# Issuing the transfers of an RWKV pair's turn from SyncE or ScalarE, by the planner's choice

## The chip, the cores and the metric

The kernel runs on one core of one Trainium2 chip. The metric is the device time of the whole program in microseconds, as the median of several runs; lower is better. The engines are TensorE (PE, with its weight load PEld), VectorE (DVE), ScalarE (ACT), GpSimd (POOL) and SyncE (SP). SyncE does no arithmetic; in the kernel before, it issues every data transfer.

## The reference

One inference step of one decoder layer, for a prompt of 1024 tokens and 8 sample tokens, width 1024, all in float32. The input is projected by `w_in`; two branches (gated linear attention with 4 heads, and RWKV-7 with 16 heads of 64) run a recurrence over the tokens; their outputs are projected, gated, added, projected again and normalized. The part that matters here is the RWKV-7 recurrence:

```python
def step(S, inp):
    rt, wt, kt, vt, kkt, at = inp
    sa = jnp.einsum('bhvk,bhk->bhv', S, -kkt)
    S = S * wt[:, :, None, :] + sa[..., None] * (kkt * at)[:, :, None, :] + vt[..., None] * kt[:, :, None, :]
    y = jnp.einsum('bhvk,bhk->bhv', S, rt)
    return S, y
...
p = jnp.einsum('btd,dn->btn', x, w_in)
...
m = (jax.nn.sigmoid(gate_a) * jnp.einsum('btc,cd->btd', o_gla, w_up_gla)
     + jax.nn.sigmoid(gate_b) * jnp.einsum('btc,cd->btd', o_rwkv, w_up_rwkv))
out = jnp.einsum('btd,de->bte', m, w_out)
y_out = _layernorm(DEEPNORM_ALPHA * x + out, ln_g, ln_b, LN_EPS)
```

## The kernel before

**Passes and blocks.** The prompt is worked in two passes (`PASS`, line 29): 512 tokens with the 8 sample tokens (as columns 256 + 264), then 512 tokens. In each pass, `blocks` (line 689) projects `w_in` block by block, 128 output columns at a time: 24 products for each column tile (8 slices of the width, each in three parts of a split into high and low halves), into one of two PSUM banks named `proj`. When the 24 are done, ScalarE or VectorE empties the bank (`evacuate`, line 730). The weights come as `wraw`, are split into `wpart` by ScalarE and VectorE, are stored in DRAM (`w`) and come back as `wpart` in the second pass. In the trace nearly every instruction has line 219, since one helper records them, so instructions are told apart by their tiles.

**A pair's turn.** The 16 RWKV heads go in 8 pairs per pass, 16 turns in all (`pair`, line 1075). The recurrence is done in chunks of 64 tokens, which needs the inverse of a triangular matrix for each chunk and head. `front` (line 1099) forms the products `GG` (tile `gg`), and then:

1. four transfers store the diagonal 32 x 32 blocks of `gg` to DRAM (`LD`, line 1178), four bring them back as one block per partition (`wide<-LD`, line 1186);
2. VectorE solves all blocks together, 62 small instructions over `X` and `Xt`;
3. four transfers store the solution (`XD<-X`, line 1198); four take off-diagonal blocks of `gg` into `L1` (shown as `L<-gg`, line 1207); four bring the solution into `XT` (line 1212) and four into `X2` (shown as `X<-XD`, line 1216). The last two need `XD` to have landed;
4. `back` (line 1219) transposes on VectorE (`X<-XT`) and takes two small products on TensorE (`big<-X,L` and `big<-X,A`) for the off-diagonal part.

That makes 24 transfers per pair, 384 in all. Then `chain` (line 1264) walks through the 8 chunks in order, with three products each on TensorE (`pch`) and copies between them on ScalarE and VectorE, and `norm` normalizes the pair's output.

**What sets the order.** All work is written as streams of operations, and `run` (line 373) acts as a list scheduler while the program is built. It keeps a clock for each engine, estimates the start of every stream's next operation (`start`, line 336) from prices (`price`, line 147) and from when its inputs are ready, and takes the one with the smallest start time less a priority. An `Engine` object (line 208) with several engines gives an operation several ways, of which `start` takes the one that ends first; `self.C` (ScalarE or VectorE) and `self.E` (VectorE or GpSimd) are of that kind. Each engine's instructions then run on the chip strictly in the order in which they were recorded, and a waiting instruction holds up all that stand behind it on its engine. A transfer is priced at 0.56 us of SyncE's clock, and its landing is estimated by `transfer` (line 202). All transfers go through `self.S`, SyncE alone.

Of the kernel before, what the change touches and what calls it, by code (L numbers as in the profile page):

```python
# [20 lines left out]
P = 128  # L21
D = 1024
# [11 lines left out]
NCH = HT // C  # L34
# [34 lines left out]
SWITCH = 0.09  # L69
# [6 lines left out]
LANDED = 0.5  # L76
BIAS = 0.1
ASIDE = 0.5

PRIO = {"evacuate": 0.7, "pair": 0.4, "turn": 0.5, "chain": 0.5, "norm": 0.1, "x": 0.7, "lora": 0.2, "rank": -0.3,  # L80
        "head": 0.3, "gate": 0.05, "w": 0.3, "out": -0.1, "state": 0, "block": 0.0}
# [7 lines left out]
HS = (slice(0, 64), slice(64, 128))  # L89
# [57 lines left out]
def price(eng, name, out, args, ins):  # L147

    n = out.free_size()
    src = [x for x in ins if x.tensor.space != PSUM] if eng == "A" else ins  # L150
    if eng == "P":
        m = args[0].free_size()
        rows, cols = tiles(name, args)
        if name == "transpose":
            return 0.112 * rows / P
        if args[0].dtype == F32R:
            return max(m / 1200, n / 2165)
        if rows == cols == P:
            return 2 * max(m, n) / 1200 + 0.005
        return 2 * (max(m, n) if cols == P else m + n) / 1200 * min(0.5 if cols == P else 0.25, rows * cols / P ** 2) + (0.01 if cols == P else 0.0)  # L160
    if eng == "S":
        return 0.56
    if eng == "A":
        extra = len(ins) - 1
        return 0.097 + n / 1200 + (0.042 if len(src) == len(ins) else 0.0) + 0.094 * extra
    wide = max([n, *(x.free_size() for x in ins)]) if name in ("tensor_reduce", "bn_stats", "bn_aggr") else n
    if eng == "V":
        if name == "tensor_tensor_scan":
            return 0.1 + n / 480
        if name in ("tensor_copy", "copy", "memset") and ins and ins[0].tensor.space != PSUM:  # L170
            wide = wide / 2
        scalars = sum(x.free_size() == 1 for x in ins[1:]) if name in ("scalar_tensor_tensor", "tensor_scalar") else 0
        return 0.068 + wide / (480 if name == "copy_predicated" else 960) + 0.06 * scalars
    if name in ("tensor_scalar", "memset"):
        return 0.08 + n / 760
    return 0.1 + n / (300 if name == "tensor_copy" else 456)
# [31 lines left out]
class Engine:  # L208
# [3 lines left out]
    def __getattr__(self, name):  # L212
        def make(out, *args, **kw):
            ins = [x for x in (*args, *kw.values()) if isinstance(x, AP)]
            ways = []
            lag, table, part, port = 0.0, None, None, ""
            for eng, handle in self._handles.items():
                call = getattr(handle, "tensor_copy" if (eng, name) == ("V", "copy") else name)
                ways.append((eng, lambda call=call: call(out, *args, **kw), price(eng, name, out, args, ins)))  # L219
                if eng in "VG" and shared(eng, name, out, ins):  # L220
                    port += eng
            if eng == "S":
                lag = transfer(out, args[0])
            elif eng == "A" and name == "activation":
                table = SETS.get(args[1])
            elif eng == "P":
                part = tiles(name, args)
            return Op(ways, out, ins, lag, table, part, port)
        return make
# [22 lines left out]
class Order:  # L252
# [4 lines left out]
    def __init__(self, nc):  # L257
        self.P, self.A, self.V, self.G, self.S, self.E, self.C = (Engine(**e) for e in (
            {"P": nc.tensor}, {"A": nc.scalar}, {"V": nc.vector}, {"G": nc.gpsimd}, {"S": nc.sync},
            {"V": nc.vector, "G": nc.gpsimd}, {"A": nc.scalar, "V": nc.vector}))  # L260
        self.tiles = (P, P)
        self.quads = {"V": {}, "A": {}}
        self.time = dict.fromkeys("PAVGS", 0.0)
        self.port = dict.fromkeys("VG", 0.0)
        self.dma = 0.0
        self.table = EXP
        self.ready, self.read = {}, {}
        self.streams = []
        self.idle, self.make, self.home, self.wait = {}, {}, {}, {}
        self.kept, self.tile = {}, {}  # L270
# [65 lines left out]
    def start(self, op):  # L336

        best = None
        for eng, fn, cost in op.ways:
            free, t = self.time[eng] + (SWITCH if eng == "P" and op.tiles != self.tiles else 0.0), 0.0  # L340
            for x in (*op.outs, *op.ins):
                at, by = self.ready.get(x.tensor.name, (0.0, None))
                if eng == "S" and by == "D" and x is op.out:
                    continue
                if by != eng:
                    at += HOP.get(by, 0.0) + (SPARE if eng == "P" and by in ("V", "A", "G") else LANDED if by == "D" else 0.0)
                elif eng != "P" and x is not op.out:
                    at += 0.13
                t = max(t, at)
            t = max(t, *(self.read.get(x.tensor.name, 0.0) for x in op.outs))  # L350
            if eng in op.port:
                free = max(free, self.port["G" if eng == "V" else "V"])
            late, t = free - t, max(t, free)
            if eng in "VA" and self.held(eng, op):
                cost += HOLD
            end = t + cost
            if len(op.ways) > 1:
                end += BIAS if eng == "V" and "A" in op.ways[0][0] else ASIDE if eng == "G" and "G" in op.port else 0.0
            if best is None or end < best[0]:
                best = end, t  # L360
                op.eng, op.fn, op.cost, op.late = eng, fn, cost, max(0.0, late)
        return best[1]
# [10 lines left out]
    def run(self):  # L373
        while self.streams:
            best, before = None, list(self.streams)
            self.urgent = self.needed()
            for s in before:
                self.advance(s)
                if s.op is not None:
                    t = self.start(s.op)  # L380
# [10 lines left out]
            _, t, s = best  # L391
            op, s.op = s.op, None
            cost = op.cost
# [2 lines left out]
                self.table = op.table  # L396
                self.nc.scalar.preload_act_table_set(self.table)  # L397
            op.fn()
            self.time[op.eng] = max(self.time[op.eng], t + cost)
            if op.eng in op.port:  # L400
                self.port[op.eng] = t + cost
            if op.eng == "P":
# [2 lines left out]
                for x, q in self.starts(op):  # L405
                    self.quads[op.eng][x is op.out, x.space] = q
            end = t + cost
            if op.eng == "S":
                self.dma = max(self.dma, end) + op.lag[0]
                end = self.dma + op.lag[1]  # L410
            for x in op.outs:
                n = x.tensor.name
                self.ready[n] = max(end, self.ready.get(n, (0.0,))[0]), "D" if op.eng == "S" else op.eng
            for x in op.ins:
                n = x.tensor.name
                self.read[n] = max(self.read.get(n, 0.0), end)
# [2 lines left out]
class Kern(Order):  # L419
# [679 lines left out]
    def front(self, c, p, st, d):  # L1099
        a, A, V, E = self.a, self.A, self.V, self.E  # L1100
        BK_, L_ = (yield from self.get("bk")), (yield from self.get("wide"))
# [3 lines left out]
        GG = gg.rearrange("p (c k h t) -> p c k h t", c=NCH, k=2, h=2)  # L1105
# [56 lines left out]
        H = NCH // 2  # L1162
# [10 lines left out]
        NU = 4 * NCH  # L1173
        LD = self.dr.tile([4, NCH, 32, 32], F32, name=f"LD{c.i}{p}")
        for q in range(2):
            b = slice(32 * q, 32 * q + 32)
            for h in range(2):
                yield self.S.dma_start(LD[2 * q + h].rearrange("c s t -> s c t"), GG[HS[h]][b, :, 0, h, b])
        L = L_.rearrange("p (s t) -> p s t", t=32)
        X_ = yield from self.get("X")  # L1180
        X = X_.rearrange("p (i t) -> p i t", t=32)
# [1 line left out]
        for q in range(4):  # L1183
            yield E.memset(X_[NU * q:NU * q + NU, q::36], 1.0)
        for q in range(4):
            yield self.S.dma_start(L_[NU * q:NU * q + NU], LD.rearrange("n c s t -> (n c) (s t)"))
        tm = yield from self.get("Xt")
        for j in range(31):
            w, ni = 31 - j, j // 4 + 1
# [5 lines left out]
        XT = (yield from self.get("XT")).rearrange("p (c h t) -> p c h t", c=NCH, h=2)  # L1195
        XD = self.dr.tile([4 * NCH, 32, 32], F32, name=f"XD{c.i}{p}")
        for q in range(4):
            yield self.S.dma_start(XD.rearrange("u (i g) t -> g u i t", g=4)[q], X[NU * q:NU * q + NU])
        self.free(X_)

        L1 = (yield from self.get("L1")).rearrange("p (x t) -> p x t", t=32)
# [1 line left out]
        H = NCH // 2  # L1203
        for h in range(2):
            for n in range(2):
                g = 2 * h + n
                yield self.S.dma_start(L1[32 * g:32 * g + 32], GG[64 * h:64 * h + 32, H * n:H * n + H, 0, h, 32:64])
        for q in range(2):
            b = slice(32 * q, 32 * q + 32)
            for h in range(2):  # L1210
                n = 2 * q + h
                yield self.S.dma_start(XT[HS[h]][b, :, h, b], XD[n * NCH:(n + 1) * NCH].rearrange("c s t -> s c t"))

        for x in range(H):
            b = slice(32 * x, 32 * x + 32)
            yield self.S.dma_start(X2[b, :, b], XD[2 * NCH + x::H].rearrange("g s t -> s g t"))
        d.AZ, d.BK, d.G, d.XT, d.v, d.bonus, d.pc, d.L, d.L1, d.X2 = AZ, BK, GG, XT, st[2], st[1], pc, L_, L1, X2

    def back(self, d):
# [577 lines left out]
```

## Time and profile before

| | |
|---|---|
| median of 3 runs | 1496.26 us (1493.49 to 1500.5) |
| the profiled execution | 1493.88 us, of which the span from first to last instruction is 1492.1 us |
| TensorE's granted clock, mean | 0.998 |
| transfers moved | 319.01 MB, mean 214 GB/s |

In the profile, a busy engine is one that executes an instruction; register and semaphore instructions and the issue of a transfer are not counted as busy. Rows with `SPq` are SyncE's issues, with the time that the issue took SyncE (not the transfer). A row "A <- B: us, times, longest" says that an instruction of engine A sat idle until one of B ended. In rows of a window, the busy time of PE, PEld, DVE, ACT and POOL is followed by the granted clock, the DMA engines' busy share and the GB/s moved.

### The profile page before, as it was taken

The page shows a single profiled execution, that of the slowest core. Times are in us where ns is not written, and L with a number is a line of the kernel's source. Part 1 is how long each engine was busy: PE and PEld are TensorE (multiplying, and loading weights), DVE is VectorE, ACT ScalarE, POOL GpSimd, SP SyncE. Part 2 cuts the span into 40 slices and gives each one's busy share as a digit, 9 for nine tenths or more (in the row PEclk, how much of TensorE's full clock was granted, in tenths as well). Part 3 has the DMA queues.
Part 4 walks back from the last instruction along what each step waited for, and adds up shares of the span by engine and source line. Part 5 has one row for each costly group of instructions (what it writes and reads, how often), then busy time and mean ns, then how long its engine had stood idle before and what let it go on. Part 6 is the DMA issues. An engine that isn't in the chain of part 4 may idle for free.

```text
span 1492.1 us, 30560 instructions
## 1 busy us (share of the span) xinstructions
PE 1466.4 (98%) x10678; PEld 1282.5 (86%) x10678; DVE 1201.9 (81%) x3159; ACT 880.1 (59%) x2221; POOL 115.5 (8%) x217
## 2 busy tenths in 40 slices
PE   9999999999999999999999999999999999999997
PEld 6998999999999999787877887787788899988786
DVE  6697889988998898979887998888777876756665
ACT  6665767767677677565754556465646746644210
POOL 1001002101120002001001010101000000000000
PEclk9999999999999999999999999999999999999999
DMA  9876697668767877675566565656554768887432
GB/s 310 282 267 207 221 314 227 218 220 302 234 220 221 297 239 241 185 237 168 165 203 175 161 199 180 181 154 171 177 172 135 234 197 258 282 300 264 143 106 85
DMA packets 211253, 319.01 MB, mean 214 GB/s; under 512 B 91683, under 2 KB 107180, under 8 KB 211100
## 3 DMA queue, kind: packets, MB, share of 16 engines
q1 hardware_dynamic: 211100, 317.06, 66.6%
q8 instruction: 85, 1.39, 0.4%
q14 instruction: 68, 0.56, 0.1%
HBM read 197.32 MB, written 118.61 MB: 212 GB/s over the span
## 4 chain that ended last, share of the span: by engine, by line
PE 83%; DVE 7%; DMA 4%; ACT 2%; issue 1%; SPq 1%; POOL 0%; POOLq 0%; DVEq 0%; ACTq 0%
PE proj L219 51%; PE big L219 22%; PE pch L219 6%; PE pY L219 5%; DVE row L219 2%; SPq L219 1%; DMA row<-o_rwkv 1%; ACT row L219 1%; DMA wraw<-w_in 1%; DVE X L219 1%; DVE wpart L219 1%; DMA wide<-LD 1%; DMA row<-state_rwkv 1%; DVE Xt L219 0%; ACT L397 0%
## 5 line engine op out<-in xcount | busy, mean ns | idle before, releaser
L219 PE MATMUL proj<-xs,wpart 128*128 128x264 f32 (+2 forms) x5640 | 1028.6, 327 | 1.2 <-DVE row L219 0.8
L219 PEld LDWEIGHTS proj<-xs,wpart 128*128 128x128 f32 x5640 | 814.4, 189 | 80.8 <-issue 10.3
L219 ACT CAST wpart<-wraw 128x512 fp32r<-128x512 f32 x210 | 130.2, 623 | 84.1 <-PE big L219 31.0
L219 DVE TENSOR_TENSOR wpart<-wraw,wpart 128x512 fp32r<-128x512 f32 x205 | 142.5, 697 | 33.4 <-ACT wpart L219 30.2
L219 DVE TENSOR_TENSOR row<-row 128x512 f32<-128x512 f32 (+10 forms) x295 | 156.8, 536 | 10.9 <-DMA row<-state_rwkv 6.2
L219 ACT ACTIVATE row<-row 128x512 f32<-128x512 f32 (+4 forms) x229 | 138.6, 610 | 26.2 <-DVE row L219 13.8
L219 POOL TENSOR_TENSOR row<-row 128x256 f32<-128x256 f32 (+7 forms) x74 | 70.3, 955 | 669.5 <-DVE row L219 232.9
L219 DVE TENSOR_TENSOR Xt<-X,wide 128x60 f32<-128x60 f32 (+24 forms) x496 | 108.4, 218 | 15.4 <-DMA wide<-LD 2.7
L219 DVE TENSOR_TENSOR X<-X,Xt 128x60 f32<-128x60 f32 (+24 forms) x496 | 106.0, 214 | 12.0
L219 ACT ACTIVATE row<-proj,omu 128x256 f32<-128x256 f32 (+1 forms) x99 | 54.3, 549 | 72.2 <-PE proj L219 71.8
L219 PE MATMUL big<-xs,wpart 128*128 128x512 f32 (+2 forms) x552 | 93.5, 324 | 0.0
L219 PEld LDWEIGHTS big<-xs,wpart 128*128 128x128 f32 x552 | 81.1, 188 | 8.7
L219 PE MATMUL big<-row 128*128 128x128 f32 (+4 forms) x464 | 86.6, 317 | 0.3 <-DVE Xt L219 0.3
L397 ACT ACT_TABLE_LOAD x64 | 82.1, 1283 | 1.1
L219 DVE SCALAR_TENSOR_TENSOR wide<-pch,pc,s0p 64x64 f32<-64x64 f32 x208 | 58.5, 281 | 28.3 <-PE pch L219 23.9
L219 DVE SCALAR_TENSOR_TENSOR row<-proj,pv,row 128x255 f32<-128x255 f32 (+1 forms) x99 | 56.3, 569 | 30.2 <-ACT tail L219 23.0
L219 ACT COPY row<-wide 64x64 f32<-64x64 f32 x240 | 57.9, 241 | 32.7 <-DVE wide L219 25.2
L219 ACT COPY wide<-pch 64x64 f32<-64x64 f32 x165 | 34.2, 207 | 65.1 <-PE pch L219 63.7
L219 PEld LDWEIGHTS big<-row 128*128 128x128 f32 (+3 forms) x464 | 60.5, 175 | 8.2 <-ACT row L219 0.8
L219 ACT COPY row<-big 128x128 f32<-128x128 f32 (+7 forms) x140 | 39.9, 313 | 41.7 <-PE big L219 40.4
L219 ACT ACTIVATE row<-proj 128x128 f32<-128x128 f32 (+4 forms) x136 | 36.9, 324 | 31.2 <-PE proj L219 30.5
L219 PE MATMUL big<-part,headsr 128*128 128x512 f32 x128 | 53.4, 418 | 1.7 <-DVE part L219 1.7
(234 smaller groups left out, 2025.8 us busy)
## 6 DMA issues: line engine op xcount, KB each, us to landing
w<-wpart SPq DMA_DIRECT2D x146, 512.0 KB
wpart<-w SPq DMA_DIRECT2D x146, 512.0 KB
wraw<-w_in SPq DMA_DIRECT2D x146, 256.0 KB
wide<-LD SPq DMA_DIRECT2D x64, 128.0 KB
wraw<-w_up_gla SPq DMA_DIRECT2D x32, 256.0 KB
wraw<-w_up_rwkv SPq DMA_DIRECT2D x32, 256.0 KB
sg<-row SPq DMA_DIRECT2D x16, 260.0 KB
row<-sg SPq DMA_DIRECT2D x16, 260.0 KB
```

The lines of the kernel that those rows point to most:

```text
L219: ways.append((eng, lambda call=call: call(out, *args, **kw), price(eng, name, out, args, ins)))
L397: self.nc.scalar.preload_act_table_set(self.table)
```

## The change

The six groups of transfers of a pair's turn are now made through `self.B`, which has two ways: `S` is SyncE's queue and `Q` is ScalarE's. The way `Q` is priced at 0.45 us on ScalarE's clock (SyncE keeps 0.56), and for the choice 0.3 us (`ASIDE_Q`) is added to its end. Whichever ends sooner by this estimate issues the transfer. Landing is estimated as before, with one shared clock of the DMA engines for both. All other transfers stay on SyncE.

```diff
+ASIDE_Q = 0.3
...
-    if eng == "S":
-        return 0.56
+    if eng in "SQ":
+        return 0.56 if eng == "S" else 0.45
...
+        self.Q = Engine(Q=nc.scalar)
+        self.B = Engine(S=nc.sync, Q=nc.scalar)
...
-            free, t = self.time[eng] + (SWITCH if eng == "P" and op.tiles != self.tiles else 0.0), 0.0
+            free, t = self.time["A" if eng == "Q" else eng] + (SWITCH if eng == "P" and op.tiles != self.tiles else 0.0), 0.0
...
-                end += BIAS if eng == "V" and "A" in op.ways[0][0] else ASIDE if eng == "G" and "G" in op.port else 0.0
+                end += ASIDE_Q if eng == "Q" else BIAS if eng == "V" and "A" in op.ways[0][0] else ASIDE if eng == "G" and "G" in op.port else 0.0
...
-            self.time[op.eng] = max(self.time[op.eng], t + cost)
+            clock = "A" if op.eng == "Q" else op.eng
+            self.time[clock] = max(self.time[clock], t + cost)
...
-            if op.eng == "S":
+            if op.eng in "SQ":
                 self.dma = max(self.dma, end) + op.lag[0]
                 end = self.dma + op.lag[1]
...
-                yield self.S.dma_start(LD[2 * q + h].rearrange("c s t -> s c t"), GG[HS[h]][b, :, 0, h, b])
+                yield self.B.dma_start(LD[2 * q + h].rearrange("c s t -> s c t"), GG[HS[h]][b, :, 0, h, b])
...
-            yield self.S.dma_start(L_[NU * q:NU * q + NU], LD.rearrange("n c s t -> (n c) (s t)"))
+            yield self.B.dma_start(L_[NU * q:NU * q + NU], LD.rearrange("n c s t -> (n c) (s t)"))
...
-            yield self.S.dma_start(XD.rearrange("u (i g) t -> g u i t", g=4)[q], X[NU * q:NU * q + NU])
+            yield self.B.dma_start(XD.rearrange("u (i g) t -> g u i t", g=4)[q], X[NU * q:NU * q + NU])
...
-                yield self.S.dma_start(L1[32 * g:32 * g + 32], GG[64 * h:64 * h + 32, H * n:H * n + H, 0, h, 32:64])
+                yield self.B.dma_start(L1[32 * g:32 * g + 32], GG[64 * h:64 * h + 32, H * n:H * n + H, 0, h, 32:64])
...
-                yield self.S.dma_start(XT[HS[h]][b, :, h, b], XD[n * NCH:(n + 1) * NCH].rearrange("c s t -> s c t"))
+                yield self.B.dma_start(XT[HS[h]][b, :, h, b], XD[n * NCH:(n + 1) * NCH].rearrange("c s t -> s c t"))
...
-            yield self.S.dma_start(X2[b, :, b], XD[2 * NCH + x::H].rearrange("g s t -> s g t"))
+            yield self.B.dma_start(X2[b, :, b], XD[2 * NCH + x::H].rearrange("g s t -> s g t"))
```

Since the planner decides, the whole order is made anew. Of the 384 transfers, 168 come to stand on ScalarE and 216 stay on SyncE; the other 947 transfers stay on SyncE too. ScalarE has 61 table loads in place of 65, and 36 copies that it did stand on VectorE now. TensorE has the same 9106 matrix instructions in another order.

The first place is SyncE's queue at the seventh pair of the second pass, after its solve; `wpart<-w` are weights that come back. Before:

```order
715 L219 DMA wpart<-w_1_8439 128x1024
716 L219 DMA wpart<-w_0_8476 128x1024
717 L219 DMA XD_15594<-X 256x1x32 x4
718 L219 DMA L_15619<-gg 32x4x32 x4
719 L219 DMA XT_167<-XD_15594 32x8x32 x4
720 L219 DMA X_173<-XD_15594 32x4x32 x4
721 L219 DMA wpart<-w_1_8528 128x1024
```

And now:

```order
705 L220 DMA wpart<-w_0_8363 128x1024
706 L220 DMA XD_15540<-X 256x1x32 x2
707 L220 DMA L_15551<-gg 32x4x32 x2
708 L220 DMA wpart<-w_1_8471 128x1024
709 L220 DMA XT_167<-XD_15540 32x8x32 x2
710 L220 DMA X_173<-XD_15540 32x4x32 x2
711 L220 DMA wpart<-w_0_8533 128x1024
```

Half of each group has left the queue, and a load of weights stands between `L` and `XT`.

The second place is ScalarE's queue at the same pair. `row<-proj,omu`, `tail<-proj` empty a projection bank, `part<-row` is the high half of a split for a head sum on TensorE. Before:

```order
1474 L219 COPY row<-row 128x256
1475 L219 ACTIVATE row<-row 128x512
1476 L219 CAST part<-row 128x512
1477 L219 COPY row<-row 128x256
1478 L219 COPY row<-big 64x2x64 x2
1479 L219 COPY row<-big 128x384 x2
1480 L219 ACTIVATE row<-proj,omu 128x512
```

And now:

```order
1543 L220 COPY tail<-proj 128x1
1544 L220 ACTIVATE row<-carry,row,pv 128x1
1545 L220 DMA XD_15540<-X 256x1x32 x2
1546 L220 DMA L_15551<-gg 32x4x32 x2
1547 L220 DMA XT_167<-XD_15540 32x8x32 x2
1548 L220 DMA X_173<-XD_15540 32x4x32 x2
1549 L220 ACTIVATE row<-row 128x512
1550 L220 ACTIVATE row<-proj,omu 128x512
1551 L220 COPY tail<-proj 128x1
1552 L220 COPY row<-row 128x256
1553 L220 CAST part<-row 128x512
```

Eight issues stand together ahead of the square, the emptying of a bank and the cast; the fifth of them must wait until `XD` has landed.

The third place is ScalarE's queue at the fourth pair of the first pass, now (before, it held no transfers); `wpart<-wraw` is the split of weights:

```order
487 L220 DMA XD_5031<-X 256x1x32 x2
488 L220 ACTIVATE row<-proj,omu 128x264
489 L220 COPY carry<-proj 128x1
490 L220 COPY tail<-proj 128x8
491 L220 DMA L_5049<-gg 32x4x32
492 L220 ACTIVATE row<-bnd,row,pv 128x1
493 L220 COPY smp<-row 128x8
494 L400 ACT_TABLE_LOAD
495 L220 ACTIVATE row<-big,pv 128x512 x2
496 L220 ACTIVATE row<-proj 128x128 x2
497 L220 DMA XT_168<-XD_5031 32x8x32
498 L220 CAST wpart<-wraw 128x512
```

Here ScalarE's other work stands between the issues, the emptying of a bank among it.

More of the change, by code (lines that the diff above doesn't have):

```diff
@@ L221, in make @@
                     port += eng
-            if eng == "S":
+            if eng in "SQ":
                 lag = transfer(out, args[0])
@@ L339, in start @@
         for eng, fn, cost in op.ways:
-            free, t = self.time[eng] + (SWITCH if eng == "P" and op.tiles != self.tiles else 0.0), 0.0
+            free, t = self.time["A" if eng == "Q" else eng] + (SWITCH if eng == "P" and op.tiles != self.tiles else 0.0), 0.0
             for x in (*op.outs, *op.ins):
                 at, by = self.ready.get(x.tensor.name, (0.0, None))
-                if eng == "S" and by == "D" and x is op.out:
+                if eng in "SQ" and by == "D" and x is op.out:
                     continue
@@ L412, in run @@
                 n = x.tensor.name
-                self.ready[n] = max(end, self.ready.get(n, (0.0,))[0]), "D" if op.eng == "S" else op.eng
+                self.ready[n] = max(end, self.ready.get(n, (0.0,))[0]), "D" if op.eng in "SQ" else op.eng
             for x in op.ins:
```

## The prediction

> **What bounds the kernel now.** I read the page's first part, then busy time by stage, then what TensorE waits for, then SyncE's rows around one turn.
>
> ```profile
> span 1492.1 us, 30560 instructions
> PE 1466.4 (98%) x10678; PEld 1282.5 (86%) x10678; DVE 1201.9 (81%) x3159; ACT 880.1 (59%) x2221; POOL 115.5 (8%) x217
> ```
>
> TensorE (PE) is busy for 1466.4 of 1492.1 us; ScalarE (ACT), which is to take on work, has 612 us free. The same by stage (width, then busy us of PE, PEld, DVE, ACT and POOL, the granted clock, the DMA share and GB/s):
>
> ```profile
> 0.00:50.00 50.00, 47.05 (x335) 38.23 (x336) 32.66 (x68) 32.87 (x77) 4.54 (x15) 1.00 0.89 307
> 50.00:1450.00 1400.00, 1384.92 (x10175) 1215.50 (x10174) 1146.98 (x3055) 845.23 (x2137) 108.21 (x199) 1.00 0.68 214
> 1450.00:1492.10 42.10, 34.42 (x173) 28.74 (x171) 22.24 (x37) 1.99 (x8) 2.77 (x3) 0.94 0.26 87
> ```
>
> PE's idle time is 25.71 us: 2.95 before 50 us, 7.68 in the last stretch (the last rows' LayerNorm), and 15.08 between. The first transfer of a turn is issued at 62 us, the last at 1219 us (rows below), so the change can reach the 15.08 us and neither end. The clock is granted in full up to 1450 us, so nothing is to be had there.
>
> A busy PE could still be a stretched PE. One piece of the second pass, where a chain's small products stand between projections (start, duration):
>
> ```profile
> 1171.26 0.38 PE L219 MATMUL pch<-wide,gg 128*128 128x128 f32 x2
> 1171.40 1.87 PE L219 MATMUL proj<-xs,wpart 128*128 128x512 f32 x7
> 1173.10 0.38 PE L219 MATMUL pch<-rh,XT 128*128 128x128 f32 x2
> 1173.24 1.40 PE L219 MATMUL proj<-xs,wpart 128*128 128x512 f32 x5
> 1174.48 0.38 PE L219 MATMUL pch<-wide,bk 128*128 128x128 f32 x2
> 1174.62 2.11 PE L219 MATMUL proj<-xs,wpart 128*128 128x512 f32 x8
> 1176.57 0.38 PE L219 MATMUL pch<-wide,gg 128*128 128x128 f32 x2
> 1176.71 1.41 PE L219 MATMUL proj<-xs,wpart 128*128 128x512 f32 x5
> ```
>
> From start to start, seven projections and a product take 1173.24 - 1171.40 = 1.84 us, five and a product 1.38 us: two more cost 0.46, so 0.23 us each and 0.23 for the product. Eight and a product should then take 2.07; from 1174.62 to 1176.71 they take 2.09, so no stall hides here. PE's work is the floor, the change leaves all its 9106 matrix instructions, and only the 15.08 us are in play, 1.0% of the time. What PE's idle time is put down to:
>
> ```profile
> PE pch L219 <- DVE wide L219: 4.4, 6, 1.8
> PE pch L219 <- DVE rh L219: 2.5, 4, 1.0
> PE big L219 <- DMA X<-XD: 1.8, 1, 1.8
> PE big L219 <- DVE X L219: 1.5, 3, 0.6
> PE proj L219 <- DVE row L219: 0.8, 1, 0.8
> PE big L219 <- DVE Xt L219: 0.3, 1, 0.3
> ```
>
> The turn's transfers are behind the third row and, through VectorE's transposes, the fourth: 3.3 us in all, in four waits. The two largest are VectorE's steps of the chain, which no transfer of a turn feeds.
>
> **The change, part by part.** First the price of an issue, by kind (count; shortest, median and longest ns), then the seventh pair's return from the solve in the second pass:
>
> ```profile
> L219 SPq DMA_DIRECT2D LD<-gg x64: 303/442/1441, 62.3 to 1169.0; - x64
> L219 SPq DMA_DIRECT2D wide<-LD x64: 302/420/1961, 69.0 to 1175.0; - x64
> L219 SPq DMA_DIRECT2D XD<-X x64: 550/568/1362, 109.7 to 1212.1; - x64
> L219 SPq DMA_DIRECT2D L<-gg x64: 586/600/640, 113.2 to 1214.7; - x64
> L219 SPq DMA_DIRECT2D XT<-XD x64: 365/451/1757, 116.0 to 1217.5; - x64
> L219 SPq DMA_DIRECT2D X<-XD x64: 388/430/1703, 120.5 to 1219.4; - x64
> ```
>
> ```profile
> 1129.61 2.57 SPq L219 DMA_DIRECT2D XD<-X  x4
> 1132.23 2.56 SPq L219 DMA_DIRECT2D L<-gg  x4
> 1134.95 1.96 SPq L219 DMA_DIRECT2D XT<-XD  x4
> 1136.95 1.87 SPq L219 DMA_DIRECT2D X<-XD  x4
> ```
>
> *Off SyncE, onto ScalarE.* The new order has 168 of the 384 issues on ScalarE: 31 LD, 27 wide, 26 XD, 29 L, 26 XT and 29 X. By the medians that is 13.7 + 11.3 + 14.8 + 17.4 + 11.7 + 12.5 = 81 us. No row here shows an issue from ScalarE; I take SyncE's price since it is the same instruction, with the longest of these rows, 1.96 us, as the upper end for one. What ScalarE loses:
>
> ```profile
> L397 ACT ACT_TABLE_LOAD x64 | 82.1, 1283 | 1.1
> L219 ACT COPY wide<-pch 64x64 f32<-64x64 f32 x165 | 34.2, 207 | 65.1 <-PE pch L219 63.7
> L219 ACT COPY wide<-big 64x256 f32<-64x256 f32 x47 | 17.3, 368 | 1.5 <-PE big L219 0.3 <-DVE wide L219 0.2
> ```
>
> There are four table loads fewer (-5.1 us), and 36 copies move to VectorE, 19 of them the chain's at 0.207 us and 17 others, for which I take 0.368: -3.9 - 6.3 = -10 us. ScalarE comes to 880 + 81 - 15 = 946 us, 63%; VectorE, at the same prices, to 1212 us, still 81%. Neither becomes the bound by its total; the cover of these 66 us is ScalarE's 612 free us. Where that cover is gone, at the moment of a burst, the second rival below has the price.
>
> *The turn gets shorter.* In the rows above SyncE issues without a pause from 1129.61 to 1138.82, 9.2 us. With halves on two engines each issues two XD (1.14 us) and two L (1.20), then must wait for XD to land, then issues two XT (0.90) and two X (0.86). The nearest landing of such a store, in the chain of work that ended last:
>
> ```profile
> 799.15 2.99 DMA LD<-gg
> 803.57 4.85 DMA wide<-LD
> ```
>
> A store lands 2.99 us after its issue starts. The second XD starts at 0.57 and lands at 3.56 us; the issuers are through with L at 2.34; so they wait 1.22 us, and the turn's issues end at 5.3 us in place of 9.2. It saves 3.9 us per pair. Before, four L in a row (2.56 us) covered that landing. What is this worth? PE has projections to do while a turn runs, and only the 3.3 us of waits above hang on it; over sixteen turns 62 us of latency are saved, and nearly all were hidden anyway. Bounds for this term: -3.3 us, if all four waits go, and 0, if what follows the transfer (VectorE's queue) is late instead. I take -2, since the one wait named DMA, 1.8 us, is the surest.
>
> *A wait put on ScalarE's queue.* The 1.22 us now also stop ScalarE. In the new order, XD, L, XT and X of that pair stand on ScalarE with nothing between; behind them stand a square and a cast that a head sum on PE needs, and the evacuation of a projection bank. In the second pass's other pairs a few of ScalarE's own rows stand among the issues. How early ScalarE comes to such evacuations now, and what SyncE had to wait for the other store:
>
> ```profile
> ACT row L219 <- PE proj L219: 125.7, 123, 3.6
> SPq L219 <- DMA LD<-gg: 4.5, 3, 2.3
> ```
>
> It stood ready before 123 of them, 1.02 us ahead on average. A stop of 1.22 us, less this lead, leaves 0.2 us per pair, 3.2 us over sixteen, and the second projection bank covers part. Bounds: 0, when all is covered, and 16 x 1.22 = 19.5 us, when each wait reaches PE in full. It is no gain, for a wait on ScalarE can only delay what stands behind it. I take +1: the price is nearer to the low end, since in PE's list above only 0.8 us stand behind the emptying of a projection bank.
>
> *The rest of the order.* All queues are planned anew from the first pair on. A new plan may hit or miss the other 11.8 us of waits in the middle. I take 0 from bounds of -11.8 and, by the same size, +11.8.
>
> Sum, against the execution profiled: 1492.1 - 2 + 1 + 0 = 1491.1 us of span. That execution took 1493.88 us in all, 1.78 around the span, and lies 2.4 below the median of the three runs, 1496.26 (1493.49 to 1500.5). The change is -1.0 us, so I predict 1495 for the median. Less than 0.5%, 7.5 us, is what a measurement of this kernel can tell from no change.
>
> The Trainium skill's page "DMA: Bandwidth & Descriptors", section "Issuing engines are not separate DMA queues", says that issuing from several engines saves only the sequencers' time for issuing, and that the transfers run on the same 16 DMA engines. By that rule my -3.9 us per turn stands and nothing more is won, so the sum would be the same.
>
> **The rivals.**
>
> *Most of the middle idle time goes (faster).* SyncE loses 81 us of issues, so loads of weights and gates queued behind a turn go out up to 3.9 us earlier, and the planner may use what is freed. For it: the 9.2 us bursts with no pause, and a projection's weights come by that queue. Against it: PE waits for no weights from a DMA in its list, and its largest waits are VectorE's. Priced at ten of the 15.08 us: 1486.
>
> *Issues from the two engines shut each other out (slower).* If descriptors for both are made by one generator, two issues that meet take turns: the turn keeps its 9.2 us, and ScalarE is held not for 4.1 us of issues but for 8.2, plus the 1.22 us of landing. On ScalarE behind it waits the evacuation of a bank that PE fills in 24 x 0.23 = 5.5 us; from there on, plus the 1.02 us of lead, PE stops: 8.2 + 1.22 - 5.5 - 1.02 = 2.9 us in each of the second pass's eight turns, 23 us: 1519. That is its upper end: in seven of the eight turns other rows of ScalarE stand among the issues, and an evacuation may be one of them, so I take half, 11.5 us: 1507. In the first pass a bank is filled sooner:
>
> ```profile
> 8.49 3.06 PE proj L219 x24
> ```
>
> 24 half-wide projections take 3.06 us, but there the order leaves at most four of ScalarE's issues in a row, 2.3 us by the medians of XD and L, 4.7 if doubled, so little is added. For it: the issues are back to back on both engines just there. Against: rows of one issuing engine can't show it, and SyncE's medians include whatever the generator costs already.
>
> The rule behind this: the Trainium skill, "Perfetto Trace Analysis", section "DMA Instruction — HWDGE (DVE, Sync)", says that the descriptor generator is shared by the issuing sequencers and locked for one at a time, and that this lock is in the profiled duration. No run here shows it yet.
>
> *It does not do what it says (no change).* The transfers are split, but a turn ends by its landings and by VectorE's queue: "DMA wide<-LD" takes 4.85 us where an issue takes 0.42. Then the -2 isn't had, and the +1 is small: 1496.
>
> **How the numbers follow.** The forecast has 0.40 and the split without effect 0.12, both within 0.5%: 0.52. Most of the middle idle time going has 0.25, all of it faster by over 0.5%. The collision has 0.23, slower by over 0.5% from 7.5 of its 23 us on. The forecast's own range, from the bounds -3.3 and the nearer part of the others, is 1489 to 1502. The range for 8 in 10 goes to 1482, where 14 of the 15.08 us are gone, and to 1512, seven tenths of the collision's upper end.
>
> **What would show it.** Right: PE busy near 1466 us; idle time between 50 and 1450 us of 10 to 20 us; "PE big <- DMA X<-XD" gone or shorter; ScalarE's 168 issues with medians as above; XD to X of a pair in about 5.3 us on each of two queues; waits of ScalarE's queue for DMA XD<-X near 1.2 us each. Issues with medians near 0.9 us in the bursts, and PE waiting for "ACT row", would show the collision. PE's idle time in the middle under 6 us would show the first rival. The forecast is wrong if PE's busy time itself changes by over 7 us: then the plan's order, not the issues, has decided.

## The result, and the profile after

The changed kernel takes 1513.29 us (median of 4 runs, 1512.16 to 1514.64), the kernel before 1498.1 us in the same comparison (1493.49 to 1500.5). The ratio is 1.0107 with a 95% interval of 1.0087 to 1.0127: slower by 15 us, where no change was forecast, and 1.3 us above the upper end of the range.

The head of the page of the changed kernel:

```profile
span 1512.3 us, 30595 instructions
PE 1476.4 (98%) x10678; PEld 1284.7 (85%) x10678; DVE 1213.1 (80%) x3194; ACT 863.6 (57%) x2179; POOL 128.8 (9%) x220
```

The span grew by 20.2 us between the two profiled executions; that is more than the 15 us of the medians, since the one before lay 4 us under its median. Half of the growth is PE's busy time, +10.0 us for the same 10678 records, and half its idle time. By stage, with the last 42 us apart as before:

```profile
0.00:50.00 50.00, 47.00 (x332) 37.86 (x333) 32.42 (x68) 32.62 (x77) 4.53 (x15) 1.00 0.86 303
50.00:1470.00 1420.00, 1394.72 (x10176) 1217.90 (x10176) 1158.46 (x3090) 828.97 (x2095) 121.48 (x202) 1.00 0.67 211
1470.00:1512.30 42.30, 34.65 (x173) 28.92 (x172) 22.25 (x37) 1.99 (x8) 2.77 (x3) 0.94 0.26 88
```

The ends are as they were (3.00 and 7.65 us idle); the middle has 25.28 us idle in place of 15.08. The clock, 1.00 over the whole middle, is not full in all of it. Two stretches of 3.4 us have half of it (third number from the end of a row):

```profile
121.80:125.20 3.40, 3.40 (x24) 3.18 (x24) 2.79 (x7) 0.14 (x1) 0.00 (x0) 0.51 0.90 308
708.80:712.20 3.40, 3.40 (x20) 2.18 (x14) 3.30 (x7) 1.99 (x6) 0.00 (x0) 0.51 1.06 388
```

The profiled execution before has no such stretch ahead of its last 42 us. If PE does half as much in them, the two explain about 3 us of the 10.0 us of busy time, an estimate. What brings such a stretch on, no run here shows. By what PE's idle time is put down to:

```profile
PE big L220 <- DVE part L220: 6.4, 10, 1.5
PE pch L220 <- DVE wide L220: 6.2, 12, 1.4
PE big L220 <- DVE X L220: 3.1, 3, 2.3
PE big L220 <- ACT row L220: 2.0, 3, 1.1
...
PE big L220 <- ACT part L220: 1.1, 2, 0.6
```

The wait for "DMA X<-XD" is gone. In its place stand many short waits for results of VectorE and ScalarE, "part" first: the split for a head sum, of which ScalarE makes the first half. Three rows of ScalarE's own waits show where it was held up; before, no row of it named one of these transfers:

```profile
ACT row L220 <- DMA XD<-X: 15.0, 4, 4.8
ACT row L220 <- DMA XT<-XD: 6.6, 3, 3.0
ACT wpart L220 <- DMA L<-gg: 6.3, 1, 6.3
```

The profile names the landing of a transfer that ScalarE issued just then; what such an idle time consists of, the order of time shows. One such place, the return of the second pass's fifth pair, on ScalarE, SyncE and PE, with VectorE's last step of the solve; other rows are left out (start, duration; ACTq is ScalarE issuing):

```profile
994.71 0.39 ACT L220 ACTIVATE row<-carry,row,pv 128x1 f32<-128x1 f32 x1
996.10 0.17 DVE L220 TENSOR_TENSOR X<-X,Xt 128x8 f32<-128x8 f32 x1
996.30 1.26 ACTq L220 DMA_DIRECT2D XD<-X  x2
996.33 2.59 SPq L220 DMA_DIRECT2D XD<-X  x2
997.66 2.18 ACTq L220 DMA_DIRECT2D L<-gg  x2
998.97 1.28 SPq L220 DMA_DIRECT2D L<-gg  x2
999.88 0.43 ACT L220 COPY row<-row 128x256 f32<-128x256 f32 x1 [4.78 <-DMA XD<-X]
...
1000.36 0.72 PE L220 MATMUL big<-row 128*128 128x128 f32 x4 [1.08 <-ACT row L220]
1000.46 0.83 ACTq L220 DMA_DIRECT2D XT<-XD  x2
1000.99 0.86 SPq L220 DMA_DIRECT2D XT<-XD  x2
1001.33 0.94 ACTq L220 DMA_DIRECT2D X<-XD  x2
```

ScalarE is done at 995.10, waits until 996.30 for VectorE to end the solve (at 996.27), issues four transfers until 999.84, and only then copies; PE stands 1.08 us for that copy. The wait here is not the one that I had foreseen, for XD's landing: it comes ahead of XD. Before, such waits and issues stood on SyncE, which computes nothing.

The price of an issue on ScalarE, by kind:

```profile
L220 ACTq DMA_DIRECT2D LD<-gg x31: 309/401/1415, 63.0 to 1181.7; - x31
L220 ACTq DMA_DIRECT2D wide<-LD x27: 319/362/994, 68.8 to 1184.8; - x27
L220 ACTq DMA_DIRECT2D XD<-X x26: 569/604/881, 172.4 to 1224.6; - x26
L220 ACTq DMA_DIRECT2D L<-gg x29: 602/630/1442, 110.5 to 1226.3; - x29
L220 ACTq DMA_DIRECT2D XT<-XD x26: 319/361/1382, 114.6 to 1229.5; - x26
L220 ACTq DMA_DIRECT2D X<-XD x29: 309/443/772, 115.3 to 1230.5; - x29
```

The medians are SyncE's of before within 0.09 us, some lower. So there is no general collision, although 145 of the 168 overlap an issue of SyncE. Single ones are stretched: above, two L at 997.66 took 2.18 us where two medians are 1.26, and SyncE's two XD beside them 2.59 us.

### The profile page after: what moved, and what is told of

Read it like the earlier page. It is cut to its first block, busy times and chain, and to the rows that moved or that the text cites. A ratio compares the mean times of both kernels' runs of the same rounds, so it can differ in the third digit from the quotient of the medians.

```text
span 1512.3 us, 30595 instructions
## 1 busy us (share of the span) xinstructions
PE 1476.4 (98%) x10678; PEld 1284.7 (85%) x10678; DVE 1213.1 (80%) x3194; ACT 863.6 (57%) x2179; POOL 128.8 (9%) x220
## 4 chain that ended last, share of the span: by engine, by line
PE 40%; DVE 6%; DMA 4%; ACT 2%; issue 1%; SPq 1%; ACTq 1%; POOL 0%; POOLq 0%; DVEq 0%
PE proj L220 21%; PE big L220 14%; PE pY L220 3%; PE pch L220 2%; DVE row L220 2%; DMA wpart<-w 1%; ACT row L220 1%; DVE wide L220 1%; DVE X L220 1%; SPq L220 1%; ACTq L220 1%; DVE Xt L220 1%; DVE part L220 1%; DMA gla_s<-row 0%; DMA wide<-LD 0%
## 5 line engine op out<-in xcount | busy, mean ns | idle before, releaser
L220 PE MATMUL proj<-xs,wpart 128*128 128x256 f32 (+2 forms) x5640 | 1032.6, 328 | 1.3 <-DVE row L220 0.8
L220 ACT ACTIVATE row<-row 128x512 f32<-128x512 f32 (+3 forms) x229 | 138.5, 610 | 30.1 <-DVE row L220 7.8
L220 DVE TENSOR_TENSOR row<-row 128x256 f32<-128x256 f32 (+9 forms) x283 | 149.3, 532 | 7.1 <-DMA row<-state_rwkv 3.0
L220 POOL TENSOR_TENSOR row<-row 128x256 f32<-128x256 f32 (+7 forms) x86 | 87.4, 1020 | 769.6 <-DVE row L220 275.7
L220 PE MATMUL big<-xs,wpart 128*128 128x512 f32 (+2 forms) x576 | 100.2, 327 | 1.3 <-ACT xs L220 0.7
L220 PEld LDWEIGHTS big<-xs,wpart 128*128 128x128 f32 x576 | 85.9, 188 | 11.6 <-DVE xs L220 0.9
L220 PEld LDWEIGHTS big<-row 128*128 128x128 f32 (+3 forms) x460 | 60.3, 176 | 11.4 <-ACT row L220 2.4
L220 ACT COPY wide<-pch 64x64 f32<-64x64 f32 x146 | 30.1, 206 | 47.0 <-PE pch L220 45.1
```

## The experiments

Every ratio is to the kernel before on the same chip, with its 95% interval. "The old order" and "the new order" mean that VectorE, PE and GpSimd have the instructions of the kernel before, or of the changed kernel, in the very same order, and ScalarE too but for the issues; only the engine that issues some transfers differs. TensorE's mean granted clock lay between 0.988 and 0.999 in the executions that the ratios rest on. It is named where a difference is small, for 0.003 of 1500 us would be 4.5 us, an estimate.

**Is it ScalarE's queue or the order?** In the first run the planner still decides as in the change, but both of its queues are SyncE's:

```diff
-        self.Q = Engine(Q=nc.scalar)
-        self.B = Engine(S=nc.sync, Q=nc.scalar)
+        self.Q = Engine(Q=nc.sync)
+        self.B = Engine(S=nc.sync, Q=nc.sync)
```

> The changed kernel's order on every engine, word for word, but SyncE issues the 168 transfers that the planner put on ScalarE. If ScalarE's queue is to blame (its issues, or the landings that it waits for), the loss of 15 us goes: 1495 to 1502. If the new order of PE, VectorE and ScalarE is to blame, it stays: 1508 to 1520, the upper end if SyncE's queue, which the planner thought freer than it is here, adds waits.

Measured: 1531.79 us, 1.0225 (1.0195 to 1.0255). Neither theory had that: slower than the changed kernel by 18 us. The second run keeps the kernel before and plans all transfers for SyncE, but issues half of each group from ScalarE:

```diff
+        self.SA = (self.S, Engine(S=nc.scalar))
-                yield self.S.dma_start(LD[2 * q + h]...
+                yield self.SA[h].dma_start(LD[2 * q + h]...
```

and likewise for the other five groups.

> The order of the kernel before on every engine, word for word, but 192 of the turn's 384 transfers (half of each group) are issued from ScalarE, at the same places of the order. If ScalarE's queue is to blame: 1508 to 1520, since here no planner made room for the issues. If the order is: 1495 to 1503.

Measured: 1501.72 us, 1.0034 (1.0023 to 1.0044): 5 us slower. That lies within the expectation that blames the order, 1495 to 1503, but the interval shows that ScalarE's issues cost something even so. Of the 17.3 us by which the first run's span exceeds the changed kernel's, 8.3 us are seen in one of PE's waits; one return on SyncE stands beside it:

```profile
PE big L220 <- DVE X L220: 11.4, 8, 2.0
```

```profile
1004.27 3.28 SPq L220 DMA_DIRECT2D XD<-X  x4
1007.61 2.57 SPq L220 DMA_DIRECT2D L<-gg  x4
1010.92 1.84 SPq L220 DMA_DIRECT2D XT<-XD  x4
1012.81 1.97 SPq L220 DMA_DIRECT2D X<-XD  x4
```

As I read it, the new order has PE's next step of the turn placed for a short return; with 10.5 us of return on SyncE, PE waits for VectorE's transposes behind it, 11.4 us in place of 3.1. A comparison of a fixed order on other queues is thus fair only to the order's own queues; the runs below that stay in the old order must be read as what ScalarE's issues cost where no room was planned for them.

**Does any new order cost as much?** Four neighbours of the kernel before, all on SyncE, with another price of an issue, which makes the whole order anew:

```diff
-        return 0.56
+        return 0.54
```

> The kernel before, all transfers on SyncE, with the planner's price of an issue at 0.54 us in place of 0.56, which makes the whole order anew for no reason of substance. If orders differ by chance and the kernel before has a lucky one, this is slower by 5 to 20 us as well; if orders of one planner are much alike, 1494 to 1502.

> As the run with 0.54, with 0.58 us. Same expectations: slower by 5 to 20 us if the old order is a lucky one among many, 1494 to 1502 if orders are much alike.

> The kernel before, all transfers on SyncE, the planner's price of an issue 0.55 us. The two runs with 0.54 and 0.58 came out 11.5 and 17.8 us slower. If the old order is a lucky one among many, this is slower too, by 5 to 20 us; if those two were unlucky, it is within 5 us of the kernel before.

> As the run with 0.55, with 0.57 us. Same expectations: 5 to 20 us slower if the old order is lucky, within 5 us if not.

And four neighbours of the changed kernel, by the handicap of ScalarE's queue:

```diff
-ASIDE_Q = 0.3
+ASIDE_Q = 0.28
```

> The changed kernel with the planner's handicap of ScalarE's queue at 0.28 us in place of 0.3, another order of the same kind. If the changed kernel's loss is the luck of its order, such orders scatter as those on SyncE alone do, 1500 to 1518 with a mean near 1510. If two issuers are worth something, their mean lies under that of the orders on SyncE alone by 3 us or more; if ScalarE's waits cost, over it by 3 or more.

> As the run with 0.28, with 0.32 us: 1500 to 1518 if the order's luck decides, and the mean of the orders with two issuers against the mean of those with one tells what the issuing is worth.

> The changed kernel with the handicap of ScalarE's queue at 0.26 us: a fourth order with two issuers. Three came out 1.1 to 1.3% slower than the kernel before, four neighbours on SyncE alone 0.0 to 1.1%. If two issuers cost by themselves, 1508 to 1520 again; if that was chance, about as likely 1497 to 1508.

> As with 0.26, with 0.34 us: 1508 to 1520 if two issuers cost by themselves; about as likely 1497 to 1508 if the other three were chance.

Two more orders have fewer issues on ScalarE, by a handicap of 1.0 (49 of its 61 belong to the return, not the 46 of the expectation), or since the planner chooses for LD and wide alone (`self.B` in those two groups, `self.S` in the other four).

> The changed kernel with the handicap at 1.0 us: 61 issues on ScalarE in place of 168, in a new order. If ScalarE's hold is the cost, it falls with the issues at the return (46 stand there), to what orders on SyncE alone show, 1497 to 1508; if not, 1510 to 1518.

> The changed kernel with the planner's choice for LD and wide alone; the return (XD, L, XT, X) stays on SyncE: 53 issues on ScalarE, in a new order. In the old order such issues cost nothing. If ScalarE's hold at the return is what the two issuers cost, this scatters as the orders on SyncE alone do, 1497 to 1515 with a mean near 1505; if any issue on ScalarE costs, 1511 to 1519.

Measured, with the count of issues on ScalarE:

| planned order | issues on ScalarE | median us | ratio (95% interval) |
|---|---|---|---|
| SyncE alone, price 0.55 | 0 | 1497.87 | 1.0003 (0.9994 to 1.0013) |
| SyncE alone, price 0.57 | 0 | 1499.49 | 1.0018 (1.0007 to 1.0029) |
| SyncE alone, price 0.54 | 0 | 1508.13 | 1.0086 (1.0058 to 1.0114) |
| SyncE alone, price 0.58 | 0 | 1514.4 | 1.0114 (1.0094 to 1.0134) |
| LD and wide by choice | 53 | 1498.0 | 0.9991 (0.9975 to 1.0007) |
| handicap 1.0 | 61 | 1496.94 | 1.0003 (0.9988 to 1.0017) |
| handicap 0.34 | 160 | 1517.59 | 1.0128 (1.0110 to 1.0146) |
| handicap 0.32 | 164 | 1516.9 | 1.0125 (1.0109 to 1.0140) |
| handicap 0.3 (the change) | 168 | 1513.29 | 1.0107 (1.0087 to 1.0127) |
| handicap 0.28 | 169 | 1517.57 | 1.0120 (1.0099 to 1.0142) |
| handicap 0.26 | 170 | 1520.47 | 1.0152 (1.0132 to 1.0173) |

Two things follow. An order's luck is worth 0.0 to 1.1% here: a price off by 0.02 us cost up to 1.1%, with nothing else changed by hand. Part of that may be the clock, for price 0.58 ran at 0.993 to 0.995 and the kernel before beside it at 0.995 to 0.999. And all five orders with 160 or more issues on ScalarE lie at 1.1 to 1.5%, while two new orders with 53 and 61 lose nothing. The five lie at 1.26% on average, the four on SyncE alone at 0.55%: 11 us apart, where 3 had been asked for (of which 2 may be the clock, 0.9955 on average against 0.9969). Luck alone would have to fall the same way five times, though these five are not five independent draws: VectorE's first 1268, 752, 209 and 217 of about 3200 instructions stand in the changed kernel's order with handicaps of 0.28, 0.32, 0.26 and 0.34. Among the orders with two issuers, the loss comes with many issues.

**What in the issues costs?** In the old order, only the issues ahead of the solve, half of LD and wide, from ScalarE; then the whole return from ScalarE (`self.SA[1]` for all of XD, L, XT and X):

> The old order, word for word; half of the transfers ahead of the solve (LD and wide, 64 in all) are issued from ScalarE, the rest from SyncE. With 192 issues on ScalarE the old order lost 5 us. Theory: ScalarE is held where the return from the solve (XD) must wait for VectorE's last step, with its other work behind it; the transfers ahead of the solve don't wait there. Then this costs 0 to 2 us: 1496 to 1499. Rival: every issue costs ScalarE alike, then a third of the loss, about 2 us, 1498 to 1500; the two touch, and the next run is the one that parts them.

> The old order, word for word; all 256 transfers of the return (XD, L, XT, X) are issued from ScalarE, none from SyncE, in place of 128. If ScalarE's hold at the return is the cost, it doubles or more, for the hold is now 8.2 us of issues: plus 10 to 25 us, 1507 to 1522. If what cost 5 us was two engines issuing at once and shutting each other out, it goes, as ScalarE issues alone: 1496 to 1501.

Measured: 0.9994 (0.9981 to 1.0007; 1496.35 us), and 1.0258 (1.0237 to 1.0279; 1535.36 us), more than expected. With the 5 us of the half-and-half run: 0, 128 and 256 issues of the return cost 0, 5 and 38 us. The expectation of a mere collision (1496 to 1501 with ScalarE issuing alone) fell. PE's waits with the whole return on ScalarE:

```profile
PE big L219 <- DVE part L219: 10.8, 9, 2.6
...
PE big L219 <- ACT part L219: 4.6, 5, 2.5
...
PE big L219 <- ACT row L219: 3.6, 9, 0.8
```

These are the same names as in the changed kernel, in an order that is the old one word for word. PE's busy time grows as well:

```profile
PE 1481.4 (97%) x10678; PEld 1286.4 (84%) x10678; DVE 1203.4 (79%) x3159; ACT 883.6 (58%) x2221; POOL 112.6 (7%) x217
```

Then each half of the return by itself:

> The old order, word for word; XD and L (128 issues) are issued from ScalarE, XT and X from SyncE. With all 256 of the return on ScalarE the old order lost 38 us. XD stands and waits for VectorE's last step of the solve, and XD and L take 4.7 us of issues. If the wait for the solve is what holds ScalarE: plus 25 to 38 us, 1522 to 1535. If the issues' own time is: 58% of 38, plus 22 us, 1515 to 1525.

> The old order, word for word; XT and X (128 issues) are issued from ScalarE, XD and L from SyncE. XT waits only for a landing that SyncE's four L cover. If the wait for the solve is what holds ScalarE: plus 0 to 8 us, 1497 to 1506. If the issues' own time is: 42% of 38, plus 16 us, 1509 to 1518.

Measured: XD and L 1.0137 (1.0121 to 1.0152; 1515.93 us), XT and X 1.0169 (1.0147 to 1.0190; 1521.88 us). The theory that the wait for the solve is the cost fell: the half without it, expected at 0 to 8 us, cost 25. The issues' own time fits better: 22 and 16 us expected, 20 and 25 measured. That the second half cost more is not shown to be the issues' doing. Its four executions had a granted clock of 0.991 to 0.998, those of XD and L 0.998 throughout, and its one at 0.998 took 1517.65 us, near the other half's 1513.83 to 1517.08. With XD and L on ScalarE, a return from the start of the first XD to the end of the last X takes 9.5 us on average of the sixteen, less than the 10.6 of the kernel before; so what costs there is, as I read it, ScalarE's other work, held up:

```profile
PE big L219 <- DVE part L219: 7.8, 7, 2.1
...
PE big L219 <- ACT row L219: 2.8, 5, 1.3
PE big L219 <- ACT part L219: 2.1, 3, 1.7
```

With XT and X on ScalarE a return takes 11.1 us, and PE waits for the transfers themselves too:

```profile
PE big L219 <- DVE X L219: 5.6, 5, 2.3
...
PE big L219 <- DMA X<-XD: 3.4, 4, 1.6
...
PE proj L219 <- ACT row L219: 3.0, 1, 3.0
```

There the coupling works both ways: ScalarE's work waits for the issues, and the issues wait for ScalarE's work. How much each has of the 25 us was not parted.

A sum over the traces orders these runs better than the theories did. It is the hold: the time from the end of ScalarE's instruction ahead of a run of issues to the start of the one behind it, in which that one may also have waited for its own input.

| from ScalarE, in the old order | loss, us | all hold, us | hold by three or more issues in a row, us |
|---|---|---|---|
| half of LD and wide | 0 | 23 | 0 |
| half of each group | 5 | 81 | 9 |
| XT and X | 25 | 50 | 22 |
| XD and L | 20 | 62 | 31 |
| the whole return | 38 | 92 | 44 |

The loss does not follow the whole hold. It follows the hold by long runs, but for the two halves, whose difference may be the clock's. In the planned orders it is alike: the five with 160 or more issues have 45 to 55 us of hold by long runs, those with 53 and 61 have 0 and 19. This was seen after the runs, and none was made to test it.

**Which part of the new order matters?** In the new order, the LD and wide issues go back to SyncE and the return stays on ScalarE; then the reverse (groups that go back are planned by a second `Engine(S=nc.sync, Q=nc.sync)`):

> The new order, word for word; the 58 issues of LD and wide that stood on ScalarE are on SyncE, the 110 of the return stay on ScalarE. With all on SyncE this order lost another 18 us. If that was the return, which then takes SyncE 9 us where the order allows 5, this run stays at 1511 to 1517; if the transfers ahead of the solve matter as well, up to 1525.

> The new order, word for word; the 110 issues of the return are on SyncE, the 58 of LD and wide stay on ScalarE. If the return decides, 1525 to 1533, as with all on SyncE; if ScalarE's hold at the return costs more than the longer return does, under 1513.

Measured: 1.0082 (1.0057 to 1.0107; 1507.5 us), under the 1511 that was expected at least, and 1.0231 (1.0205 to 1.0256; 1530.12 us), as expected if the return decides. The return is what the new order needs on two queues; LD and wide on ScalarE bring nothing, if anything they cost, for the first interval meets that of the changed kernel.

## Why the prediction was wrong

**What bounds the kernel: right, but read too strictly.** PE's work is the floor. "Only the 15.08 us are in play" held for a gain, not for a loss: PE's busy time grew by 10.0 us with the same instructions. About 3 us of it are the two stretches at half clock, which I had left out because the clock was full before; the rest I take for stops too short to part two modelled matrix products, which count as busy. That part was not measured by itself. I named a change of busy time by over 7 us as the sign of the plan's order. That was wrong: the old order with the return on ScalarE has 1481.4 us, 15.0 more, at most 5 of them from three stretches at half clock.

**Issues on ScalarE: right in size.** 81 us were worked out; the issues' durations in the trace sum to about 88. The table loads went as said, 38 copies moved in place of 36, and ScalarE's busy time is 863.6 us without issues.

**The turn gets shorter: too large.** From the first XD to the end of the last X a return takes 9.0 us on average (10.6 before), not 5.3 in place of 9.2. The halves do not start together, an issue waits for the work ahead of it, and SyncE sends other loads in between. Of PE's gain, taken as -2 us, the two rows behind it show -0.2: "DMA X<-XD" went from 1.8 us to nothing, but "DVE X" rose from 1.5 to 3.1.

**A wait on ScalarE's queue: the step that failed.** I took +1 us, from bounds of 0 and 19.5, because ScalarE stood ready 1.02 us ahead of a projection's end on average and PE waited only 0.8 us for the emptying of a bank. Three errors are in it. The lead of 1.02 us is the mean over the 123 times that ScalarE sat idle ahead of an evacuation; it made 283 (`row<-proj`), so most had no such lead. I counted only the landing's 1.22 us, and called the 66 us of issues covered by ScalarE's 612 free us; but at twelve places four to eight issues in a row stop ScalarE for 1.6 to 6.3 us, and free time elsewhere doesn't cover that. And I priced the evacuations alone; what came late was the short chain from ScalarE over VectorE to PE that makes "part": in the old order, PE's wait for "DVE part" is 1.7 us with SyncE alone, 2.9 with half of LD and wide on ScalarE, and 4.7 to 10.8 with issues of the return there. In the changed kernel it is 6.4, of which the same order has 3.6 with all issues on SyncE. ("DVE wide" is no such sign: it stands at 6.2 now, and at 5.9 in the order with 53 issues, which lost nothing.) Summed over the trace, the time from the end of ScalarE's instruction ahead of a run of issues to the start of the one behind is about 107 us in the changed kernel, 27 of it before the first issue starts. I had 81 + 16 x 1.22 = 101: the sum of the hold was met, in part by luck, since those 27 us lie ahead of the issues and the 1.22 us were meant behind them. Its price for PE was not foreseen. In the old order that price, taken as +1, is 5 to 38 us when issues of the return are among those on ScalarE, by experiment. In the changed kernel it can't be read alone, since the order changed as well.

**The rest of the order: the second step that failed.** I took 0 from -11.8 and +11.8. Four neighbours on one queue cost 0.5, 2.7, 13 and 17 us (the ratios by 1498 us), and none gained. A new order was worth about +8 us, not 0; how much of the change's 15 us is this luck stays open, between none and most.

**The rivals.** The collision ended on the right side at 1507, but not by its mechanism: the issues' medians hardly changed, and the durations of all issues of the turns sum to about 200 us on both queues, 205 on one queue before. The lock of the descriptor generator that the Trainium skill names ("Perfetto Trace Analysis", section "DMA Instruction — HWDGE (DVE, Sync)") is at most seen in single pairs of issues, as the 2.18 us above. The rule of the Trainium skill's "DMA: Bandwidth & Descriptors", section "Issuing engines are not separate DMA queues", that several issuing engines save only issue time, agrees with what was gained, 1.6 us per return. Most idle time going, and no effect, did not happen.

## What to carry to other kernels

In this kernel an engine that computes was a poor place for issues that come several in a row: its queue is in order, and the cost is what stands behind them, not the engine's share of busy time and not the sum of its issues. In a kernel that is full on one engine, look at what that engine is fed with at that very place. And before a change to a planner is judged, measure what an equal, empty change of its numbers does: here up to 1.1%.

## What the runs showed that was not expected

ScalarE issues a transfer while instructions ahead of it in its order still compute. At the sixth pair of the second pass, XT stands behind the cast in the order, and X behind the copy of "tail":

```profile
1071.08 0.62 ACT L220 CAST part<-row 128x512 fp32r<-128x512 f32 x1
1071.22 0.37 ACTq L220 DMA_DIRECT2D XT<-XD  x1
1071.64 0.69 ACT L220 ACTIVATE row<-proj,omu 128x512 f32<-128x512 f32 x1
1071.69 0.89 ACTq L220 DMA_DIRECT2D X<-XD  x2
...
1072.22 0.15 ACT L220 COPY tail<-proj 128x1 f32<-128x1 f32 x1
```

XT's issue (1071.22 to 1071.59) lies within the cast (to 1071.70), and X's begins before the copy ahead of it. So one issue between long instructions is nearly free: the 56 that stand alone in the changed kernel hold ScalarE for 0.3 us each on average, the twelve runs of four or more for 3.5 us. That fits the 64 issues of LD and wide that cost nothing.
